# Decoder layer on one core: the gate slots' ring, the tile of the meta rows' sums, and the order around two operand splits

## The chip, the cores and the metric

The kernel runs on one core of a Trainium2 chip. The metric is the device time of one execution in microseconds (us); the time of a kernel is the median of its runs. Engines are named as in the profile: PE is TensorE, DVE is VectorE, ACT is ScalarE, POOL is GpSimd, SP is SyncE, whose queue issues most transfers.

## The reference

One layer of a hybrid decoder on 1024 tokens and 16 meta tokens put in front (T = 1040, D = 1024, feed-forward width 2816), all float32. Cut to what matters:

```python
h = layer_norm(concatenate([meta, x]), in_ln_g, in_ln_b)
z = h @ w_in + b_in          # q | k | v | conv input | 2 x 1024 gate columns
a = swa_sink_attention(q, k, v, sinks, rel_bias)      # window 128, 8 heads, 16 meta keys
y_attn = a @ w_attn_proj                              # 512 -> 1024
c = silu(layer_norm(causal_dwconv(c_val * sigmoid(c_gate), conv_dw, conv_dw_b), ...))
y_conv = c @ w_conv_proj                              # 512 -> 1024
mixed = sigmoid(g_attn) * y_attn + sigmoid(g_conv) * y_conv
h = layer_norm(alpha * h + mixed @ w_out, ln1_g, ln1_b)
u, g = split(causal_dwconv(h @ ffn_w_up, ffn_dw, ffn_dw_b))      # 3 taps
f = (gelu(g) * u) @ ffn_w_down
h = layer_norm(alpha * h + f, ln2_g, ln2_b);  return h[16:]
```

The three-tap convolution of the feed-forward part needs two columns ahead of the first output token, so the kernel carries U = 1026 columns through the second half: the last two meta rows and the 1024 tokens.

## The kernel before, in words

Every matrix product is made in three matmuls: each operand is split into a high part (a cast to the matmul's format, on ACT) and a low part (operand less high part, on DVE, or on POOL where a split isn't urgent), and hi·hi, hi·lo and lo·hi are added up in PSUM (`split`, L268 and L271; `product`, L297, L301 and L302). In the profile a cast with a following `TENSOR_TENSOR` of the same shape is such a split.

The stages, with their place in the profiled span: layer norm and transposes of the input (to about 50 us); the tiles of `w_in`, with attention and the depthwise convolution in between (to about 416); the **projection** (416 to 506); the **output rows** (506 to 605), w_out with residual, layer norm and transposes back; the **joint** to the feed-forward part (605 to 628); the up product (to about 1000) and the down product. All of it is one stream of instructions for each engine, laid down when the program is built by a scheduler that goes by priorities (`rank`) and by the order of dependences; `after(a, b)` and `line` force an order. A wait at the head of an engine's stream holds all that stands behind it.

*Projection.* `for m in range(KC)` makes the 128 output channels of tile m for four groups g of columns (258, 256, 256, 256). A group has two branches of 12 matmuls: attention (operand OA, PSUM tag "mm", three banks) and convolution (operand OC, tag "t", two banks). `merge` then loads both gates of the group from DRAM (tensor `sgd`) into a gate slot on SP's queue, multiplies: L1121 reads and frees the attention bank, L1122 the conv bank, L1123 adds them, and L1128 (ACT) and L1129 (DVE) write the split result into RHC or RHO; L1129 is the slot's last reader. `gslot` hands out the slots: the first four lie in the array FA, then a ring of four in the array OB. The gate loads of a later group therefore wait for the L1129 of the group that had the slot before.

*Meta rows.* The two meta columns of mixed are too few to be worth a matmul. L1125 stores them in `pair`, and `two_rows(k)` adds `pair` times row block k of w_out (128x1024, `wo_raw[k]`) to two sums, one for each meta row: on ACT for k = 0 (L1082), and for k = 1 to 7 by two DVE instructions (L1084). The sums lie in FA (5120 to 6143) and OB (2064 to 3087). Row blocks 0 to 3 of w_out are loaded into FA at the offsets `W_AT`, 4 into FA and 5 into OB, 6 and 7 into buffers `wr`. Places for row blocks 0, 2 and 3 are gate slots before, and the weights of the next m (`wr<-in_w_ab_dram`, split by L268 and by L271 on DVE) go over the same queue.

*Output rows.* `out_rows(i)` makes the tokens of row i in the order 3, 7, 2, -1 (the meta rows), 6, 0, 4, 1, 5, in two halves of 512; L1278 adds the residual and frees the bank, L1300 normalizes, and `turn` (L1314 on PE, L1324 on ACT) transposes the row after the first half of the next one. Between rows, a table `work` lists the splits and sums of operands for the feed-forward part: `split_of` and `form_t2` to `form_t4` make the operands of a product (L1215 the cast, L1220 the low part, L1224 sums), and `w_first(n)` draws n weight operands from the generator `up_weights` (L1362 sums, `wsplit`: L1344 the cast, L1345 the low part).

*Feed-forward.* The up product is made in 2x2 blocks with seven products instead of eight (B11, B21, BT2, BT4, BT1, BT3, B22; PSUM tiles px, pz, px, pw, py, px, py). Tile c = 0 goes in two passes, tokens of the second half first, so that it can begin before all rows are there; its second pass and the splits it needs are the joint. `copy` (L1543, ACT) empties px so that the next product in px can start. The first weight operands lie in W2, which has a pool of its own.

Of the kernel before, what the change touches and what calls it, by code (L numbers as in the profile page):

```python
# [23 lines left out]
F = mybir.dt.float32  # L24
R = mybir.dt.float32r
# [4 lines left out]
P = 128  # L30
D = 1024
# [5 lines left out]
U = T - U0  # L37
# [62 lines left out]
def tile_hybrid_layer(  # L100
# [19 lines left out]
    def after(ins, first):  # L120

        tc.add_manual_dep(ins.ins, first.ins.name, mybir.DependencyInfo(
            mybir.DependencyClass.NoSync, mybir.DependencyReason.SCHED_ONLY), reason="order of work")
# [14 lines left out]
    arena = ctx.enter_context(tc.tile_pool(name="arena", bufs=1, side="left"))  # L138
    dpool = ctx.enter_context(tc.tile_pool(name="scratch", bufs=1, space=bass.MemoryType.DRAM))

    FA = arena.tile([P, 6144], F, name="FA")
    RHC = arena.tile([P, 8320], R, name="RHC")
    RHO = arena.tile([P, 8320], R, name="RHO")
    OB = arena.tile([P, 4 * U + 64], F, name="OB")

    v1d = dpool.tile([NH, J_LEN], F, name="v1d")
    vd = dpool.tile([P, NH, J_LEN], F, name="vd")
# [119 lines left out]
    def split(raw, hi, lo, quick=False, behind=None):  # L267
        ins = nc.scalar.copy(hi, raw)  # L268
        if behind is not None:
            after(ins, behind)  # L270
        return (nc.vector if quick else nc.gpsimd).tensor_tensor(lo, raw, f32(hi), OP.subtract)  # L271
# [437 lines left out]
    for q4 in range(2):  # L709
        ps = pat.tile([P, 512], F, name="ps_v4", tag="t", bufs=2)  # L710
        for i in range(4):
            c = NMETA + (q4 * 4 + i) * P
# [306 lines left out]
    for g in range(3):  # L1019
# [4 lines left out]
    tmp_stack.close()  # L1024
    rx_p = ctx.enter_context(tc.tile_pool(name="rx", bufs=1, side="right", reuse_waits="tile"))
    RX = rx_p.tile([P, 2112], R, name="RX")
    w2_stack, wo_stack = ExitStack(), ExitStack()
    W2 = w2_stack.enter_context(tc.tile_pool(name="w2", bufs=1, side="right", reuse_waits="tile")).tile(
        [P, 2048], R, name="W2")
    wo_p = wo_stack.enter_context(tc.tile_pool(name="rw", bufs=1, side="right", reuse_waits="tile"))  # L1030
    RW = wo_p.tile([P, 2048], R, name="RW")
    RT = OB[:, 0:2048]


# [35 lines left out]
    nc.vector.memset(f32(sel), 0.0)  # L1070
    for t in range(2):
        nc.vector.memset(f32(sel[:, 3 * t:3 * t + 1]), 1.0)
    two_sum = [FA[:, 5120:6144], OB[:, 2064:3088]]
    two_parts = [[OC[:, (2 * t + hl) * D:(2 * t + hl + 1) * D] for hl in range(2)] for t in range(2)]
    wo_raw = {}

# [11 lines left out]
    g_next = [0]  # L1088

    GS = [(FA, i * 516) for i in range(4)]  # L1090
    GS += [(OB, i * 516) for i in range(4)]
    W_AT = (2048, 3072, 0, 1024)

    def gslot():
        i = g_next[0]
        t, o = GS[i if i < 4 else 4 + i % 4]
        g_next[0] += 1
        return t[:, o:o + 516].rearrange("p (i n) -> p i n", i=2)

# [2 lines left out]
    for m in range(KC):  # L1102
        hi, lo = weights([P, KC, P], lambda raw: load(raw, w_ab[m]))

        def branch(i, g, tag, bufs):
            a, b = PG[g]
            ps = pat.tile([P, 512], F, name="ps_p", tag=tag, bufs=bufs)
            rhs = (oo, conv)[i]
            product(ps[:, :b - a], [(hi[:, 4 * i + k], lo[:, 4 * i + k], rhs(k, 0, a, b), rhs(k, 1, a, b))
                                    for k in range(4)])  # L1110
            return ps[:, :b - a]

        def merge(g, psa, psb):
            a, b = PG[g]
            n = b - a
            with rank(RK_EVAC):
                t = gslot()[:, :, :n]
                ins = load(t, dram(sgd, m * P * U + a, [[U, P], [KC * P * U, 2], [1, n]]))

                ta, tb = t[:, 0], t[:, 1]  # L1120
                nc.vector.scalar_tensor_tensor(ta, ta, 1.0, psa, OP.add, OP.mult)  # L1121
                nc.vector.scalar_tensor_tensor(tb, tb, 1.0, psb, OP.add, OP.mult)  # L1122
                nc.vector.tensor_tensor(ta, ta, tb, OP.add)  # L1123
                if g == 0:
                    nc.scalar.mul(pair[:, m, 0:2], ta[:, 0:2], 0.5)  # L1125
                v = ta[:, n - 256:].rearrange("p (t x) -> p t x", t=2)
                h = mixed2(g, m, 0)
                last_act = nc.scalar.mul(h, v, 0.5)  # L1128
                nc.vector.scalar_tensor_tensor(mixed2(g, m, 1), v, 0.5, f32(h), OP.mult, OP.subtract)  # L1129
            return ins, last_act  # L1130

        if m < KC - 1:
            for g in range(4):
                last_gate, last_act = merge(g, branch(0, g, "mm", 3), branch(1, g, "t", 2))
        else:
            pa = [branch(0, g, "mm", 3) if g < 3 else branch(0, g, "s", 2) for g in range(4)]
            for g in range(4):
                last_gate, last_act = merge(g, pa[g], branch(1, g, "t", 2))
        if m in (2, 3):
            raw = (FA[:, 4096:5120], OB[:, 3088:4112])[m - 2]  # L1140
            load(raw, w_out_v[m + 2])
            prep_wo(m + 2, raw, last_act)
        if m < 4:
            early.append(FA[:, W_AT[m]:W_AT[m] + 1024])
            wo_raw[m] = early[m]
            after(load(early[m], w_out_v[m]), last_gate)
        if m > 1:
            with rank(RK_PROJ + 3000):
                two_rows(m - 2)
# [41 lines left out]
    lined, high = [], []  # L1191
# [136 lines left out]
    RING = [RHO[:, i * 1024:(i + 1) * 1024] for i in range(4)]  # L1328
    RING += [None] * 4
    RING += [RHO[:, 6208 + i * 1024:6208 + (i + 1) * 1024] for i in range(2)]  # L1330
    ring_next = [0]

    def wsplit(src):
        i = ring_next[0]
        ring_next[0] += 1
        if i < 2:
            t = W2[:, i * 1024:(i + 1) * 1024]
        else:
            i = (i - 2) % len(RING)
            if RING[i] is None:  # L1340
                RING[i] = wsp_p.tile([P, D], R, name="ws", tag=("whi", "wlo")[i % 2])
            t = RING[i]
        hi, lo = t[:, 0:512], t[:, 512:1024]
        nc.scalar.copy(hi, src)  # L1344
        ins = nc.vector.tensor_tensor(lo, src, f32(hi), OP.subtract)  # L1345
        if pinned_w[0]:
            line(ins)
        elif ring_next[0] <= 12:
            after(ins, formed[0])
        return hi, lo  # L1350
# [7 lines left out]
    def up_weights():  # L1358


        def tt(*x):
            ins = nc.vector.tensor_tensor(*x)  # L1362
            if pinned_w[0]:
                line(ins)

        rows = w_rows(0)
        for c in range(FC):
            a11, a12, a21, a22 = rows
            yield wsplit(a11)
            yield wsplit(a12)  # L1370
            p4 = wsplit(a22)
            tt(a22, a21, a22, OP.add)
            tt(a21, a11, a21, OP.subtract)
            tt(a11, a22, a11, OP.subtract)
            yield wsplit(a11)
            yield p4
            yield wsplit(a22)
            tt(a22, a12, a11, OP.subtract)
            yield wsplit(a21)
            p3 = wsplit(a22)  # L1380
            if c + 1 < FC:
                rows = w_rows(c + 1)
            yield p3
# [17 lines left out]
    def edges():  # L1401
        with rank(RK_TURN):
# [5 lines left out]

    ahead = []
    work = {0: [(w_first, 2), (split_of, 1, B11), (split_of, 1, B21), (split_of, 1, B22)],  # L1410
            4: [(w_first, 3), (split_of, 1, BT2), (form_t4, 1)],
            1: [(form_t3, 1), (split_of, 0, B11, EARLY), (form_t2, 0, EARLY), (w_first, 5)],
            5: [(w_first, 6)]}
    for i in (3, 7, 2, -1, 6, 0, 4, 1, 5):
        if i == -1:
            out_rows(i)
            continue
        rows = out_rows(i, ahead, work.get(i, ()))
        ahead = [None, (i, *rows)] if i == 3 else [(i, *rows)]
        if i == 3:  # L1420
            two_rows(7, rows[2])
        if i == 7:
            for a, (hi, lo) in zip(two_sum, two_parts):
                after(split(a, hi, lo, True), rows[2])
        if i == 0:
            form_t2(1)
        if i == 4:
            split_of(1, BT4)
            split_of(1, BT1)
            edges()  # L1430
        if i == 1:
            split_of(1, BT3)
            split_of(0, B21, EARLY)
            form_t3(0, EARLY)
            form_t4(0, EARLY)
# [1 line left out]


    ps_stack.close()
    wo_stack.close()  # L1440
    up_stack = ExitStack()
    pup = up_stack.enter_context(tc.tile_pool(name="pup", bufs=1, space=PSUM, reuse_waits="tile"))
    ft_next = [0]
# [56 lines left out]
    last_mm, copied = [], []  # L1500
    for c in range(FC):
        if c == 1:
            w2_stack.close()
            sums_p = ctx.enter_context(tc.tile_pool(name="sums", bufs=1, side="right", reuse_waits="tile"))
            RXF, SM1 = (sums_p.tile([P, 2048], F, name=n) for n in ("raw", "sums"))
            for i in range(FC):
                SM[i] = [(OB[:, 2048:4096], SM1)[i % 2][:, h * 1024:(h + 1) * 1024] for h in range(2)]
        V4, X, Z, Y = (pup.tile([P, 1024], F, name=n, tag=n) for n in ("pw", "px", "pz", "py"))
        passes = ((1,), (0,)) if c == 0 else ((0, 1),)
        for subs in passes:  # L1510
# [5 lines left out]
            def at(t, a=a):  # L1516
                return t[:, 254 + a:254 + b]
# [23 lines left out]
            def copy(*x):  # L1541
                with rank(RK_CHAIN):
                    copied.append(nc.scalar.copy(*x))  # L1543

            prod(B11, X, True)
            copy(u13[:, a:b], at(X))
            prod(B21, Z, True)
            if last and c not in (0, FH + 1):
                sums_load(c - 1 if c <= FH else c - 2)
# [277 lines left out]
```

## Time and profile before

| what | value |
|---|---|
| time, median of 3 runs | 1251.87 us (1250.74 to 1251.91) |
| time of the profiled execution | 1253.26 us |
| its span, first to last instruction | 1251.2 us |
| granted TensorE clock, mean | 0.998 |
| PE busy | 1235.7 us, 99% of the span |
| DVE busy | 1092.1 us, 87% |
| ACT busy | 588.7 us, 47% |
| POOL busy | 13.0 us, 1% |
| DMA | 212.10 MB, mean 170 GB/s |

The profile is of one execution. A row of a timeline is: start, duration, engine, line, operation, written tile `<-` read tiles, shape, and in square brackets the idle time of the engine before the row and what released it. DVE and ACT rows overlap a little: the next instruction starts before the last one's record ends, so distances from start to start are shorter than durations. A row of the list of waits is: engine, what it was about to do, what it waited for, us in total, times, longest.

### The profile page before, as it was taken

What the parts mean: (1) busy time and instruction counts of PE and PEld (TensorE: products, weight loads), DVE (VectorE), ACT (ScalarE), POOL (GpSimd) and SP (SyncE); (2) the same over time, 40 slices, a digit from 0 to 9 for tenths busy, and PEclk for the clock granted to TensorE, in tenths of its full rate; (3) what the DMA queues carried; (4) which work ended last, traced back from release to release, by engine and by line L of the source; (5) the groups of instructions that cost most, each with busy time, mean ns of one, the idle gap of its engine ahead of it and who ended that gap; (6) DMA issues with size and microseconds to landing.
All of it is one profiled execution on the core that took longest, in us unless ns stands there. A gap on an engine that the chain in (4) does not pass through costs nothing.

```text
span 1251.2 us, 21661 instructions
## 1 busy us (share of the span) xinstructions
PE 1235.7 (99%) x8514; PEld 1172.0 (94%) x8514; DVE 1092.1 (87%) x1887; ACT 588.7 (47%) x1052; POOL 13.0 (1%) x11
## 2 busy tenths in 40 slices
PE   9999999999999999999999999999999999999997
PEld 8999999999999999888899999999999998888885
DVE  7899989999978778658899999998899986995697
ACT  7522245554566222345565555554555554544330
POOL 0000000000000000100000000000000000000000
PEclk9999999999999999999999999999999999999999
DMA  7294633323244555232146555453464568988722
GB/s 280 67 305 115 184 105 95 104 83 103 68 139 132 175 158 150 84 115 86 68 144 203 181 199 203 177 212 132 156 219 175 197 224 315 393 321 295 252 85 84
DMA packets 98231, 212.10 MB, mean 170 GB/s; under 512 B 12867, under 2 KB 38019, under 8 KB 98002
## 3 DMA queue, kind: packets, MB, share of 16 engines
q1 hardware_dynamic: 86362, 199.65, 47.3%
q10 hardware_dynamic: 11768, 11.08, 2.7%
q8 instruction: 66, 1.08, 0.4%
q14 instruction: 35, 0.29, 0.1%
HBM read 150.30 MB, written 62.70 MB: 170 GB/s over the span
## 4 chain that ended last, share of the span: by engine, by line
PE 90%; DVE 4%; DMA 3%; issue 1%; ACT 1%; SPq 0%; DVEq 0%
PE px L1531 14%; PE py L1531 9%; PE ps_x L1673 9%; PE ps_z L1673 7%; PE ps_z L301 7%; PE ps_z L297 7%; PE ps_z L302 7%; PE pw L1531 5%; PE pz L1531 5%; PE ps_z L513 2%; PE ps_w L302 2%; PE ps_w L297 2%; PE ps_w L301 2%; PE ps_p L297 2%; PE ps_p L302 2%; PE ps_p L301 2%
## 5 line engine op out<-in xcount | busy, mean ns | idle before, releaser
L666 DVE SCALAR_TENSOR_TENSOR FA<-cin,cols,FA 128x1026 f32<-128x1026 f32 x120 | 152.5, 1280 | 0.2
L301 PE MATMUL ps_z<-RHC,whi 128*128 128x384 f32 (+2 forms) x324 | 104.3, 322 | 0.0
L301 PE MATMUL ps_z<-RHO,whi 128*128 128x384 f32 (+2 forms) x324 | 104.3, 322 | 0.0
L297 PE MATMUL ps_z<-RHC,whi 128*128 128x384 f32 (+2 forms) x324 | 104.0, 321 | 0.0
L302 PE MATMUL ps_z<-RHO,wlo 128*128 128x384 f32 (+2 forms) x324 | 103.9, 321 | 0.0
L297 PE MATMUL ps_z<-RHO,whi 128*128 128x384 f32 (+2 forms) x324 | 103.9, 321 | 0.0
L302 PE MATMUL ps_z<-RHC,wlo 128*128 128x384 f32 (+2 forms) x324 | 103.7, 320 | 0.0
L268 ACT CAST whi<-wr 128x1024 fp32r<-128x1024 f32 x37 | 38.9, 1050 | 73.8 <-PE ps_z L301 48.6
L1345 DVE TENSOR_TENSOR RHO<-wr,RHO 128x512 fp32r<-128x512 f32 x92 | 61.9, 683 | 6.1 <-ACT RHO L1344 6.0
L1344 ACT CAST RHO<-wr 128x512 fp32r<-128x512 f32 x92 | 55.2, 619 | 24.7 <-DVE wr L1362 11.2
L297 PEld LDWEIGHTS ps_z<-RHO,whi 128*128 128x128 f32 x324 | 61.0, 188 | 0.5 <-issue 0.3
L302 PEld LDWEIGHTS ps_z<-RHO,wlo 128*128 128x128 f32 x324 | 61.0, 188 | 0.4
L297 PEld LDWEIGHTS ps_z<-RHC,whi 128*128 128x128 f32 x324 | 61.1, 188 | 0.3
L301 PEld LDWEIGHTS ps_z<-RHO,whi 128*128 128x128 f32 x324 | 61.0, 188 | 0.3
L301 PEld LDWEIGHTS ps_z<-RHC,whi 128*128 128x128 f32 x324 | 61.0, 188 | 0.1
L302 PEld LDWEIGHTS ps_z<-RHC,wlo 128*128 128x128 f32 x324 | 60.9, 188 | 0.1
L1362 DVE TENSOR_TENSOR wr<-wr 128x512 f32<-128x512 f32 x88 | 59.9, 681 | 0.2
L673 ACT ACTIVATE FA<-ps_z,cols 128x384 f32<-128x384 f32 (+1 forms) x48 | 26.0, 541 | 47.6 <-PE ps_z L302 43.0
L1543 ACT COPY FA<-px 128x514 f32<-128x514 f32 (+2 forms) x23 | 13.2, 573 | 72.4 <-PE px L1531 72.4
L271 DVE TENSOR_TENSOR wlo<-wr,whi 128x1024 fp32r<-128x1024 f32 x35 | 42.6, 1217 | 4.6 <-ACT whi L268 4.5
L1344 ACT CAST ws<-wr 128x512 fp32r<-128x512 f32 x60 | 36.2, 619 | 18.1 <-DVE wr L1362 10.9
L1531 PE MATMUL px<-OA,RHO 128*128 128x258 f32 (+1 forms) x336 | 43.7, 279 | 0.8 <-ACT OB L1543 0.8
(473 smaller groups left out, 3520.9 us busy)
## 6 DMA issues: line engine op xcount, KB each, us to landing
wr<-in_w_up_dram SPq DMA_DIRECT2D x44, 512.0 KB, 4.5
wr<-in_w_z_dram SPq DMA_DIRECT2D x30, 512.0 KB, 4.0
fd<-FA SPq DMA_DIRECT2D x44, 256.0 KB, 2.5
OB<-in_w_down_dram SPq DMA_DIRECT2D x19, 512.0 KB, 4.8
qt<-qd SPq DMA_DIRECT2D x28, 256.0 KB, 3.6
sgd<-FA ACTq DMA_DIRECT2D x32, 192.0 KB, 4.0
td<-OB SPq DMA_DIRECT2D x12, 512.0 KB
sums<-fd SPq DMA_DIRECT2D x12, 512.0 KB, 7.4
```

The lines of the kernel that those rows point to most:

```text
L268: ins = nc.scalar.copy(hi, raw)
L271: return (nc.vector if quick else nc.gpsimd).tensor_tensor(lo, raw, f32(hi), OP.subtract)
L297: ins = nc.tensor.matmul(ps, ah, bh, start=i == 0, stop=False)
L301: nc.tensor.matmul(ps, ah, bl, start=False, stop=False)
L302: last = nc.tensor.matmul(ps, al, bh, start=False, stop=i == n - 1)
L666: nc.vector.scalar_tensor_tensor(acc[c], cin[:, j:j + U], wc, acc[c], OP.mult, OP.add)
L673: nc.scalar.activation(t, ps, AF.Tanh, bias=bcol(14 + i), scale=0.5)
L1344: nc.scalar.copy(hi, src)
L1345: ins = nc.vector.tensor_tensor(lo, src, f32(hi), OP.subtract)
L1362: ins = nc.vector.tensor_tensor(*x)
L1531: ins = nc.tensor.matmul(o, x[:, ks], bmat(sub, q, hl, k), start=first and k + j == 0, stop=k == 3 and j == 2, skip_group_check=not first)
L1673: nc.tensor.matmul(banks[i], l[:, ts], r[:, ws], start=first and a and x + k == 0, stop=z and x == len(ops) - 1 and k == 2, skip_group_che ...
```

## The change

- The sums of the meta rows get tiles of their own, in a pool `two` that lies next to the pool of RW. FA and OB no longer hold them.
- The ring of gate slots in OB has five slots, not four; OB loses its last 64 columns. The places of w_out's row blocks in FA move by 16, so that none overlaps a first gate slot but those of row blocks 2 and 3.
- W2 has no space from the start. When the sums have been split (after row 7), the pool `two` is closed, and a pool `w2` with W2 takes its space. RW's stack, W2's now too, is closed at c = 1.
- In row 4's list of work, `w_first(3)` is called twice. The generator yields once more (None) for c = 0 after its three sums, so that the first call ends there, the split for BT2 comes next, and the split of the weight sum after it.
- In the joint, the cast for BT1 is ordered behind the copy from px that follows product B11.

```diff
-    OB = arena.tile([P, 4 * U + 64], F, name="OB")
+    OB = arena.tile([P, 4 * U], F, name="OB")
...
-    w2_stack, wo_stack = ExitStack(), ExitStack()
-    W2 = w2_stack.enter_context(tc.tile_pool(name="w2", bufs=1, side="right", reuse_waits="tile")).tile(
-        [P, 2048], R, name="W2")
+    wo_stack, two_stack = ExitStack(), ExitStack()
     wo_p = wo_stack.enter_context(tc.tile_pool(name="rw", bufs=1, side="right", reuse_waits="tile"))
     RW = wo_p.tile([P, 2048], R, name="RW")
+    two_p = two_stack.enter_context(tc.tile_pool(name="two", bufs=1, side="right", reuse_waits="tile"))
...
-    two_sum = [FA[:, 5120:6144], OB[:, 2064:3088]]
+    two_sum = [two_p.tile([P, D], F, name=f"two{t}") for t in range(2)]
...
     GS = [(FA, i * 516) for i in range(4)]
-    GS += [(OB, i * 516) for i in range(4)]
-    W_AT = (2048, 3072, 0, 1024)
+    GS += [(OB, i * 516) for i in range(5)]
+    W_AT = (2064, 3088, 0, 1024)
...
-        t, o = GS[i if i < 4 else 4 + i % 4]
+        t, o = GS[i if i < 4 else 4 + (i - 4) % 5]
...
-            raw = (FA[:, 4096:5120], OB[:, 3088:4112])[m - 2]
+            raw = (FA[:, 4112:5136], OB[:, 3072:4096])[m - 2]
...
-    ring_next = [0]
+    ring_next, W2 = [0], []
...
         if i < 2:
-            t = W2[:, i * 1024:(i + 1) * 1024]
+            t = W2[0][:, i * 1024:(i + 1) * 1024]
...
             tt(a11, a22, a11, OP.subtract)
+            if c == 0:
+                yield None
             yield wsplit(a11)
...
-            4: [(w_first, 3), (split_of, 1, BT2), (form_t4, 1)],
+            4: [(w_first, 3), (split_of, 1, BT2), (w_first, 3), (form_t4, 1)],
...
         if i == 7:
             for a, (hi, lo) in zip(two_sum, two_parts):
                 after(split(a, hi, lo, True), rows[2])
+            two_stack.close()
+            W2.append(wo_stack.enter_context(tc.tile_pool(name="w2", bufs=1, side="right", reuse_waits="tile")).tile(
+                [P, 2048], R, name="W2"))
...
     ps_stack.close()
-    wo_stack.close()
...
         if c == 1:
-            w2_stack.close()
+            wo_stack.close()
...
             copy(u13[:, a:b], at(X))
+            if c == 0 and last:
+                after(high[2], copied[-1])
```

Line numbers of the changed kernel are one lower than before from the meta rows to the output rows (L1084 is L1083, L1121 is L1120), and L1543 is L1546.

How the streams move, at the three places that matter for the prediction. In the orders, ACT's casts read COPY, and DVE's instruction with a scalar and a tensor reads TENSOR_SCALAR.

**Projection, SP's queue.** Before, behind the first gate loads: gates of m = 2 (groups 0 and 1), weights of a later m, gates of groups 2 and 3, then w_out row block 2, and the same again up to the weights ahead of row block 3.

```order
L111 DMA OB<-sgd 128x2x258
L111 DMA OB<-sgd 128x2x256
L111 DMA wr<-in_w_ab_dram 128x1024
L111 DMA OB<-sgd 128x2x256 x2
L111 DMA FA<-in_w_out_dram 128x1024
L111 DMA OB<-sgd 128x2x258
L111 DMA OB<-sgd 128x2x256
L111 DMA wr<-in_w_ab_dram 128x1024
```

After, the gates of group 0 have gone out earlier, and the queue reads:

```order
L111 DMA wr<-in_w_ab_dram 128x1024 x2
L111 DMA OB<-sgd 128x2x256 x3
L111 DMA FA<-in_w_out_dram 128x1024
L111 DMA wr<-in_w_ab_dram 128x1024
L111 DMA OB<-sgd 128x2x258
L111 DMA OB<-sgd 128x2x256 x3
L111 DMA FA<-in_w_out_dram 128x1024
```

The loads of row blocks 2 and 3 now stand behind three gate loads with no weight load between them; a weight load waits for the L271 that frees its buffer.

**Projection, DVE.** Before, from group 1's first multiply in m = 2 (the pair L1084 is row block 2):

```order
L1121 TENSOR_SCALAR OB<-OB,ps_p 128x256
L1129 TENSOR_SCALAR RHO<-OB,RHO 128x2x128
L1122 TENSOR_SCALAR OB<-OB,ps_p 128x256
L1123 TENSOR_TENSOR OB<-OB 128x256
L1121 TENSOR_SCALAR OB<-OB,ps_p 128x256
L1129 TENSOR_SCALAR RHC<-OB,RHC 128x2x128
L1084 TENSOR_SCALAR FA<-FA,pair 128x1024
L1084 TENSOR_SCALAR OB<-FA,pair,OB 128x1024
L1122 TENSOR_SCALAR OB<-OB,ps_p 128x256
L1121 TENSOR_SCALAR OB<-OB,ps_p 128x256
L1122 TENSOR_SCALAR OB<-OB,ps_p 128x256
```

After, from the same multiply:

```order
L1120 TENSOR_SCALAR OB<-OB,ps_p 128x256
L1083 TENSOR_SCALAR two_4560<-FA,pair,two_4560 128x1024
L1083 TENSOR_SCALAR two_4561<-FA,pair,two_4561 128x1024
L1128 TENSOR_SCALAR RHO<-OB,RHO 128x2x128
L1121 TENSOR_SCALAR OB<-OB,ps_p 128x256
L1120 TENSOR_SCALAR OB<-OB,ps_p 128x256
L1122 TENSOR_TENSOR OB<-OB 128x256
L1121 TENSOR_SCALAR OB<-OB,ps_p 128x256
L1122 TENSOR_TENSOR OB<-OB 128x256
```

The pair stood between the multiplies of group 2 and now stands between those of group 1, one group earlier.

**Row 4, DVE.** Before, around the low part for BT2 (OC):

```order
L1345 TENSOR_TENSOR RHO<-wr,RHO 128x512
L1362 TENSOR_TENSOR wr<-wr 128x512 x3
L1345 TENSOR_TENSOR RHO<-wr,RHO 128x512
L1220 TENSOR_TENSOR OC<-OB,OC 128x1024
L1224 TENSOR_TENSOR FA<-OB,FA 128x1024
L1278 TENSOR_TENSOR OB<-ps_w,OB 128x512
```

After:

```order
L1344 TENSOR_TENSOR RHO<-wr,RHO 128x512
L1361 TENSOR_TENSOR wr<-wr 128x512 x3
L1219 TENSOR_TENSOR OC<-OB,OC 128x1024
L1344 TENSOR_TENSOR RHO<-wr,RHO 128x512
L1223 TENSOR_TENSOR FA<-OB,FA 128x1024
L1277 TENSOR_TENSOR OB<-ps_w,OB 128x512
```

The low part of OC and the low part of the weight sum (RHO) have changed places; ACT's order of their casts is as before.

**Joint, ACT.** Before, from the cast for BT2 (OA from OB) on; then those for BT4, BT1 (RX) and BT3:

```order
L1215 COPY OA<-OB 128x1032
L1215 COPY OA<-FA 128x1032
L1215 COPY RX<-FA 128x1024
L1215 COPY OA<-FA 128x1024
L1543 COPY OB<-px 128x258
L1344 COPY RHO<-wr 128x512
```

After:

```order
L1214 COPY OA<-OB 128x1032
L1214 COPY OA<-FA 128x1032
L1546 COPY OB<-px 128x258
L1214 COPY RX<-FA 128x1024
L1214 COPY OA<-FA 128x1024
L1343 COPY RHO<-wr 128x512
```

The copy from px now goes ahead of the casts for BT1 and BT3. Behind this place, in tile c = 1, the first table load and Gelu of the feed-forward part stand ahead of the copy from px of that tile, not behind it, and on PE a few matmuls of the next m's first attention branch go ahead of the last conv branch of m = 1, 2 and 3.

## The prediction

> **What bounds the kernel now.** I read the page's head first, then the list of what TensorE (PE) waits for over the whole run, then the timelines of PE, VectorE (DVE) and ScalarE (ACT) around the waits that lie in changed places.
>
> ```profile
> span 1251.2 us, 21661 instructions
> PE 1235.7 (99%) x8514; PEld 1172.0 (94%) x8514; DVE 1092.1 (87%) x1887; ACT 588.7 (47%) x1052; POOL 13.0 (1%) x11
> PE ps_p L297 <- DVE OB L1122: 2.2, 2, 1.5
> PE ps_h L463 <- DVE xn L427: 1.4, 1, 1.4
> PE ps_w L537 <- DVE sel L1070: 1.1, 1, 1.1
> PE px L1531 <- ACT OB L1543: 0.8, 1, 0.8
> PE ps_s L830 <- DMA qt<-qd: 0.8, 1, 0.8
> PE ps_h L1314 <- DVE OB L1300: 0.6, 1, 0.6
> PE ps_z L510 <- ACT FA L469: 0.3, 1, 0.3
> ```
>
> PE is busy 99% of the span and the change leaves its matmuls as they are. So nothing counts but PE's waits, 7.2 us in seven groups, and waits that the change puts in. Three groups lie where instructions move: the projection's (2.2), the joint's (0.8) and one row's transposes (0.6). No other can go.
>
> **Projection: two late bank releases.** The starts of PE's matmuls tell what the two waits cost.
>
> ```profile
> 465.22 0.28 PE L302 MATMUL ps_p<-OA,wlo 128*128 128x256 f32 x1
> 466.26 0.39 PE L297 MATMUL ps_p<-OC,whi 128*128 128x256 f32 x1 [0.76 <-DVE OB L1122]
> 472.88 0.28 PE L301 MATMUL ps_p<-OA,whi 128*128 128x258 f32 x1
> 474.64 0.39 PE L297 MATMUL ps_p<-OC,whi 128*128 128x256 f32 x1 [1.48 <-DVE OB L1122]
> 449.55 1.28 DVE L1084 SCALAR_TENSOR_TENSOR FA<-FA,pair 128x1024 f32<-128x1024 f32 x1 [2.80 <-DMA FA<-in_w_out_dram]
> 450.75 1.28 DVE L1084 SCALAR_TENSOR_TENSOR OB<-FA,pair,OB 128x1024 f32<-128x1024 f32 x1
> 462.73 1.28 DVE L1084 SCALAR_TENSOR_TENSOR FA<-FA,pair 128x1024 f32<-128x1024 f32 x1 [1.13 <-DMA FA<-in_w_out_dram]
> 469.62 3.10 DVE L1084 SCALAR_TENSOR_TENSOR FA<-FA,pair 128x1024 f32<-128x1024 f32 x1
> 469.14 2.50 POOL L271 TENSOR_TENSOR RW<-OB,RW 128x1024 fp32r<-128x1024 f32 x1 [11.04 <-ACT RW L268]
> 442.65 6.88 DMA FA<-in_w_out_dram
> 457.01 5.69 DMA FA<-in_w_out_dram
> ```
>
> A matmul of 256 columns follows the last by about 0.12 (below), so the waits cost 466.26 - 465.22 - 0.12 = 0.92 and 474.64 - 472.88 - 0.12 = 1.64, 2.56 together. Both end on L1122, which frees a conv bank (two of them), and L1122 stood behind a pair of meta sums (L1084, 1.20 start to start). The pair of w_out block 3 began at 462.73, when its load landed 5.69 after its issue at 457.01. The pair of block 4 needed no load, but its first half lay beside GpSimd's (POOL) 2.50 us split and took 3.10, not 1.28.
>
> **What the change moves there.** With five gate slots, group 0 of the next m finds a free slot, so each gate load needs the group before the one that it needed; the sums' own tiles let w_out block 0 load beside the gates. The w_out loads queue on SyncE (SP) behind gate loads, and come earlier:
>
> ```profile
> 437.45 0.28 PE L297 MATMUL ps_p<-OC,whi 128*128 128x256 f32 x1
> 441.79 0.42 DVE L1129 SCALAR_TENSOR_TENSOR RHC<-OB,RHC 128x256 fp32r<-128x256 f32 x1
> 448.52 0.28 PE L297 MATMUL ps_p<-OC,whi 128*128 128x256 f32 x1
> 459.67 0.28 PE L297 MATMUL ps_p<-OC,whi 128*128 128x256 f32 x1
> ```
>
> Those three PE rows begin the eighth branch of m 1, 2 and 3; 448.52 - 437.45 = 11.07 for 96 matmuls is 0.115 each. Before, block 2's load left at 442.65, just after L1129 of m 1's group 3 ended (441.79 + 0.42). Now the last gate load ahead of it needs L1128 (the same line) of m 1's group 2. By the new order that stands right behind the first multiply of group 3, which is ready when the seventh branch ends (437.45): 437.45 + 0.4 + 0.4 = 438.3, and 0.9 more for two issues (442.65 is 0.44 after 442.21) makes 439.2. Landing 5.69 to 6.88 later: 444.9 to 446.1.
>
> The pair itself stands one group earlier in DVE's order, between the two multiplies of group 1. Behind it wait L1128 (0.42 by L1129's row) and the multiply L1121 (as small), which frees group 1's conv bank, and PE wants that for the conv branch of group 3. That now follows six matmuls of the next attention branch: 448.52 + 6 x 0.12 = 449.2. So block 2's pair must begin by 449.2 - 2.40 - 0.84 = 446.0, and but for 0.1 at the late end it does. It ends by 447.3 to 448.5; seven short instructions later, at most 0.42 each (450.2 to 451.4), a slot is free for m 3, and block 3's load leaves 0.9 after that, 451.1 to 452.3, and lands 456.8 to 459.2. Its limit: seven matmuls ahead, 459.67 + 0.84 - 3.24 = 457.3. PE waits 0 to 1.9; I take 0.5, below the middle, since a load that leaves earlier meets fewer gate loads. Block 4's pair shows no wait for a load. It now starts when m 4's third branch is done and multiplied, 466.26 - 0.92 + 0.4 = 465.8, and even stretched by 3.10 - 1.28 = 1.82 it ends at 470.0; the bank is wanted at 472.88 less the 0.92 that no longer is lost, 472.0, and 0.84 of work lies between. No wait. Blocks 5 to 7 have no PE wait before, and each step comes no later. Sum: -2.56 + 0.5 = **-2.1** (bounds -2.56 and -0.6).
>
> W2, in the sums' old space, is written only when the sums are split: its two casts move on ACT to behind row 3's transposes. By the row of three below they are 0.57 each, 1.1 together, ahead of row 7's transposes, and PE shows no wait for those: nothing; without that cover up to 1.1.
>
> **Row 4's transposes.**
>
> ```profile
> 578.05 1.08 ACT L1215 CAST OC<-OB 128x1024 fp32r<-128x1024 f32 x1
> 578.99 1.70 ACT L1344 CAST RHO<-wr 128x512 fp32r<-128x512 f32 x3
> 580.72 0.69 DVE L1345 TENSOR_TENSOR RHO<-wr,RHO 128x512 fp32r<-128x512 f32 x1 [1.32 <-ACT RHO L1344]
> 581.33 1.22 DVE L1220 TENSOR_TENSOR OC<-OB,OC 128x1024 fp32r<-128x1024 f32 x1
> 586.21 0.81 DVE L1300 TENSOR_SCALAR OB<-OB,mv,sd 128x1024 f32<-128x1024 f32 x1
> 587.16 1.06 PE L1314 MATMUL ps_h<-cols,OB 128*128 128x128 f32 x8 [0.58 <-DVE OB L1300]
> ```
>
> DVE idles 1.32 for the third ACT cast, then makes OC's low part (1.22, of which 0.08 overlaps, as in the pairs above), and L1300 comes late for PE. The added yield splits the work differently, and OC's low part now goes first, into that idle time: its cast is done at 579.13. L1300 then ends 1.1 earlier, at 586.21 + 0.81 - 1.1 = 585.9, before PE is ready for it (587.16 - 0.58 = 586.6). The wait of 0.58 goes: **-0.6**, bounds -0.58 and 0.
>
> **The joint.**
>
> ```profile
> 617.89 1.59 PE L1531 MATMUL pz<-RHO,W 128*128 128x258 f32 x12
> 620.32 1.69 PE L1531 MATMUL px<-OA,RHO 128*128 128x258 f32 x12 [0.83 <-ACT OB L1543]
> 618.01 1.05 ACT L1215 CAST RX<-FA 128x1024 fp32r<-128x1024 f32 x1
> 619.91 0.36 ACT L1543 COPY OB<-px 128x258 f32<-128x258 f32 x1
> 620.28 1.22 DVE L1220 TENSOR_TENSOR OA<-FA,OA 128x1032 fp32r<-128x1032 f32 x1
> 621.42 1.21 DVE L1220 TENSOR_TENSOR RX<-FA,RX 128x1024 fp32r<-128x1024 f32 x1
> ```
>
> PE's product px waits 0.83 for ACT's copy, which stands behind two casts of 0.95. Now the copy goes ahead of them, at 618.0, and px starts when pz is done, 617.89 + 12 x 0.12 = 619.3. But the next product needs the low part that DVE makes from 620.28 to 621.5; it runs 11 matmuls from then, 621.55 + 1.33 = 622.9, and the one after it needs RX's low part, now behind an inserted 258-column sum, 0.42 like L1129: 621.42 + 0.42 + 1.21 = 623.0. Before, it began at 620.32 + 24 x 0.12 = 623.2 and took its second matmul, the first that needs the low part, at 623.35. **-0.4**: DVE is late next. Bounds -0.83 and 0.
>
> Sum: -2.1 - 0.6 - 0.4 = -3.1. The profiled execution took 1253.26 (its span and 2.06 around it) and would take 1250.2; the three runs' median is 1.39 below it, and I take the same waits to be in it, so 1251.87 - 3.1 = **1248.8**.
>
> **A rule against it.** In the up-projection's second tile the order of ACT changes: the copy from px, which came first, now follows a table load and a Gelu.
>
> ```profile
> 630.40 0.59 ACT L1543 COPY OB<-px 128x514 f32<-128x514 f32 x1 [0.17 <-PE px L1531]
> 631.01 1.28 ACT L1461 ACT_TABLE_LOAD   x1
> 632.31 0.63 ACT L1461 ACTIVATE FA<-FA 128x512 f32<-128x512 f32 x1
> 632.94 1.59 PE L1531 MATMUL px<-OA,RHO 128*128 128x258 f32 x12
> ```
>
> Load and Gelu took 632.31 - 631.01 + 0.63 = 1.93; begun at 630.40 - 0.17 - 0.57 = 629.7 (the cast just ahead moves behind them too) they end at 631.6 and the copy at 632.2. PE wants px at 632.94 - 0.4 = 632.5: no wait. The Trainium skill ("ScalarE: Activation LUTs", section "What ACT_TABLE_LOAD costs") gives a switch 1283 ns and a drain of 1380 ns. The trace agrees on the 1.28 and shows no drain behind it, as the Gelu starts 0.02 after the load's end; by the page's drain the copy would end 1.38 later, at 633.6, PE would wait 1.1, and the sum would be -2.0.
>
> **The rivals.**
> - The w_out loads land at the slow end. The load of block 3 then costs PE 1.9, block 2's 0.1, and the joint gives nothing: -2.56 + 2.0 - 0.6 = -1.2, 1250.7. For it: the two landings seen differ by 1.2. Against: both met gate loads issued just ahead. Chance 0.20.
> - Slower: the pairs now stand ahead of a bank release that PE wants sooner. Place: L1083 of blocks 2 and 3. Each us that a landing takes beyond 6.8 (block 2) or 5.6 (block 3, by the middle of its issues, 451.7) is PE's. At 10 us from issue, block 2 costs 439.2 + 10 - 446.0 = 3.2 and block 3 451.7 + 10 - 457.3 = 4.4; with -2.56, -0.6 and -0.4, +4.0: 1255.9. It decides from 8.0 us on, where the sum is nought. For it: three gate loads go just ahead. Against: no landing above 6.88 seen. Chance 0.11.
> - The copy of the second tile holds PE up. If a stretch as long as the load's own 1.28 lies between load and Gelu, the copy ends at 633.5 and PE waits 1.0: -3.1 + 1.0, 1249.8. The Gelu's start at 632.31 speaks against it; that the load stood behind the copy before, where a stall cost PE nothing, leaves it open. Chance 0.04. (The skill's drain, above, is this rival.)
> - The change doesn't reach PE: the loads are held by another item of SP's queue, the waits move but don't shrink, 1251.5. For it: only 3 us of 1251 can go at all. Chance 0.08.
>
> **How the numbers follow.** My forecast has 0.57. A measurement of this kernel tells about 0.2%, 2.5 us, so faster means below 1249.4: 0.54 of the forecast and 0.05 of the first rival make 0.59. Slower, above 1254.4, is the second rival's 0.11. The rest, 0.30, is within. The range's low end is all three waits gone, -2.56 - 0.58 - 0.83 = -4.0, and 0.9 for the spread of runs (1250.74 to 1251.91): 1247.0. Its high end takes the first rival and part of the no-effect case: 1251.2.
>
> **What would show it.** Right: PE's list without L1121 in the projection, or with one wait under 1 on block 3; none on the transposes' L1299; DVE's pairs of blocks 2 and 3 beginning near 445.5 and 457.9; px at the joint near 619.3 with a wait on DVE behind it. Wrong: landings above 7 us, a PE wait on L1121 in m 2 as well as m 3, a px wait at 632.

## The result, and the profile after

The changed kernel took 1249.31 us, median of 15 runs (1248.54 to 1250.80), beside 15 runs of the kernel before with a median of 1252.70. The ratio is 0.9973, 95% interval [0.9966, 0.9981]: 3.4 us faster.

The list of PE's waits of the changed kernel, whole run (columns as before: us in total, times, longest):

```profile
PE ps_h L463 <- DVE xn L427: 1.4, 1, 1.4
PE ps_w L537 <- DVE sel L1069: 1.1, 1, 1.1
PE pw L1534 <- DVE OA L1219: 0.4, 1, 0.4
PE ps_s L830 <- DMA qt<-qd: 0.4, 1, 0.4
PE ps_z L510 <- ACT FA L469: 0.3, 1, 0.3
```

The projection's two waits (2.2), the transposes' (0.6) and the copy's (0.8) are gone; one of 0.4 on the low part in OA is new. The wait on `qt` shrank by 0.4 too, at a place that the change doesn't touch. The weight load that stands just ahead of the first instruction on SP's queue that the change moves comes 0.65 earlier already (first row before, second after):

```profile
398.99 0.34 SPq L111 DMA_DIRECT2D wr<-in_w_ab_dram  x1
398.34 0.35 SPq L111 DMA_DIRECT2D wr<-in_w_ab_dram  x1
```

So I take 0.65 of the 4.1 between the two spans (1251.2 and 1247.1) as difference from one execution to the next, and times of this profile are to be read with 0.65 added when they are set against those of before.

Projection, timelines of SP, DVE and POOL:

```profile
438.20 0.46 SPq L111 DMA_DIRECT2D FA<-in_w_out_dram  x1
450.69 0.46 SPq L111 DMA_DIRECT2D FA<-in_w_out_dram  x1
444.65 2.48 DVE L1083 SCALAR_TENSOR_TENSOR two<-FA,pair,two 128x1024 f32<-128x1024 f32 x2 [1.54 <-DMA FA<-in_w_out_dram]
455.98 2.48 DVE L1083 SCALAR_TENSOR_TENSOR two<-FA,pair,two 128x1024 f32<-128x1024 f32 x2
465.00 2.18 DVE L1122 TENSOR_TENSOR OB<-OB 128x258 f32<-128x258 f32 x1
467.45 2.48 DVE L1083 SCALAR_TENSOR_TENSOR two<-FA,pair,two 128x1024 f32<-128x1024 f32 x2
464.30 2.60 POOL L271 TENSOR_TENSOR RW<-OB,RW 128x1024 fp32r<-128x1024 f32 x1 [8.88 <-DVE wlo L271]
```

The loads of blocks 2 and 3 leave at 438.20 and 450.69, some 4 and 6 us earlier than before. Block 2's pair still waits for its load on DVE, and as in the profile before it doesn't hold PE up; block 3's pair, which held PE up before, finds its data. Block 4's pair takes 2.48: what now lies beside GpSimd's split is the small add L1122, 2.18 long instead of some 0.4.

Row 4, DVE:

```profile
576.16 1.22 DVE L1219 TENSOR_TENSOR OC<-OB,OC 128x1024 fp32r<-128x1024 f32 x1
577.56 0.69 DVE L1344 TENSOR_TENSOR RHO<-wr,RHO 128x512 fp32r<-128x512 f32 x1 [0.19 <-ACT RHO L1343]
581.91 0.81 DVE L1299 TENSOR_SCALAR OB<-OB,mv,sd 128x1024 f32<-128x1024 f32 x1
```

OC's low part fills what was an idle stretch of 1.32; 0.19 of it is left.

Joint, PE, ACT and DVE:

```profile
615.35 1.73 PE L1534 MATMUL px<-OA,RHO 128*128 128x258 f32 x12
616.92 0.28 PE L1534 MATMUL pw<-OA,RHO 128*128 128x258 f32 x1
617.58 1.58 PE L1534 MATMUL pw<-OA,RHO 128*128 128x258 f32 x11 [0.38 <-DVE OA L1219]
614.12 0.38 ACT L1546 COPY OB<-px 128x258 f32<-128x258 f32 x1
616.30 1.22 DVE L1219 TENSOR_TENSOR OA<-FA,OA 128x1032 fp32r<-128x1032 f32 x1
617.78 1.21 DVE L1219 TENSOR_TENSOR RX<-FA,RX 128x1024 fp32r<-128x1024 f32 x1
```

The copy comes in time and px starts without a wait. The next product stops after one matmul until the low part in OA ends at 617.52.

Tile 1, ACT and PE:

```profile
625.83 1.28 ACT L1464 ACT_TABLE_LOAD   x1
627.13 0.63 ACT L1464 ACTIVATE FA<-FA 128x512 f32<-128x512 f32 x1
627.66 0.57 ACT L1546 COPY OB<-px 128x514 f32<-128x514 f32 x1
628.73 1.59 PE L1534 MATMUL px<-OA,RHO 128*128 128x258 f32 x12
```

The copy ends at 628.23, 0.5 before PE's next product in px.

### The profile page after: what moved, and what is told of

It reads as the page before. It is cut to its first block, busy times and chain, and to the rows that moved or that the text cites. A ratio compares the mean times of both kernels' runs of the same rounds, so it can differ in the third digit from the quotient of the medians.

```text
span 1247.1 us, 21668 instructions
## 1 busy us (share of the span) xinstructions
PE 1235.2 (99%) x8514; PEld 1172.2 (94%) x8514; DVE 1093.1 (88%) x1887; ACT 588.8 (47%) x1052; POOL 12.7 (1%) x11
## 4 chain that ended last, share of the span: by engine, by line
PE 94%; DVE 3%; DMA 1%; issue 1%; ACT 0%; SPq 0%; DVEq 0%
PE px L1534 14%; PE py L1534 9%; PE ps_x L1678 9%; PE ps_z L1678 7%; PE ps_z L301 7%; PE ps_z L297 7%; PE ps_z L302 7%; PE pw L1534 5%; PE pz L1534 5%; PE ps_p L302 2%; PE ps_p L297 2%; PE ps_p L301 2%; PE ps_w L302 2%; PE ps_w L297 2%; PE ps_w L301 2%; PE ps_z L513 2%
## 5 line engine op out<-in xcount | busy, mean ns | idle before, releaser
L1361 DVE TENSOR_TENSOR wr<-wr 128x512 f32<-128x512 f32 x88 | 60.0, 682 | 0.2
L271 DVE TENSOR_TENSOR wlo<-wr,whi 128x1024 fp32r<-128x1024 f32 x35 | 42.6, 1216 | 4.6 <-ACT whi L268 4.5
L1546 ACT COPY FA<-px 128x514 f32<-128x514 f32 (+2 forms) x23 | 13.1, 570 | 70.7 <-PE px L1534 70.6
L1344 DVE TENSOR_TENSOR ws<-wr,ws 128x512 fp32r<-128x512 f32 x60 | 40.4, 685 | 4.4 <-ACT ws L1343 4.3
```

## The experiments

**The ring and the pool alone.** The whole change without the two reorderings:

```diff
-            if c == 0:
-                yield None
...
-            4: [(w_first, 3), (split_of, 1, BT2), (w_first, 3), (form_t4, 1)],
+            4: [(w_first, 3), (split_of, 1, BT2), (form_t4, 1)],
...
-            if c == 0 and last:
-                after(high[2], copied[-1])
```

> The ring of five, the sums' own pool and W2 in its space, without the two reorderings in row 4 and at the joint. My theory (three places, each worth its PE wait): both PE waits on L1121 in the projection are gone, the waits of 0.6 on L1299 and of 0.8 on the copy from px stay, and the time falls by 2.6 us (1.0 more than a fifth of the whole remains at the other two places): ratio 0.9979. Rival A (the reorderings are what counts): the projection's waits shrink by less than 1, ratio above 0.9992. Rival B (places work on each other: with the projection earlier, DVE is late elsewhere): a new PE wait of over 0.5 between 500 and 630 us, ratio above 0.9985.

Ratio 0.9980 [0.9971, 0.9989]. From the list of PE's waits:

```profile
PE px L1532 <- ACT OB L1544: 0.9, 1, 0.9
...
PE ps_h L1313 <- DVE OB L1299: 0.6, 1, 0.6
```

No wait in the projection, both others as before, no new one: my theory's figures.

**The reorderings alone**, on the kernel before (the same lines, put in).

> The two reorderings alone, on the kernel before. My theory: the projection keeps its two PE waits (2.2 us in the list of waits), the wait of 0.6 on the transposes goes, the one of 0.8 on the copy from px becomes one of 0.4 on the low part in OA; the time falls by 1.0 us: ratio 0.9992. Rival A: it falls by 2.5 or more. Rival B (nothing at these places reaches the end): no change, ratio 1.0000, and the end of the feed-forward part doesn't move.

Ratio 0.9987 [0.9978, 0.9996]. The interval alone can't part my 0.9992 from rival A (2.5 us, a ratio of 0.998); the waits can. From the list of PE's waits:

```profile
PE ps_p L297 <- DVE OB L1122: 1.5, 1, 1.5
...
PE pw L1533 <- DVE OA L1220: 0.4, 1, 0.4
```

The transposes' wait is gone and the copy's has turned into 0.4 on OA, as expected. In the projection one wait was there in this execution, not two. The 1.5 is block 4's; block 3's hangs on when a load lands. The two parts' effects, 0.20% and 0.13%, add up to the whole 0.27% within their intervals.

**A ring of four in the changed kernel.**

```diff
-    GS += [(OB, i * 516) for i in range(5)]
+    GS += [(OB, i * 516) for i in range(4)]
...
-        t, o = GS[i if i < 4 else 4 + (i - 4) % 5]
+        t, o = GS[i if i < 4 else 4 + (i - 4) % 4]
```

> The whole change, but with a ring of four gate slots. If the ring is what brings the loads of w_out blocks 2 and 3 forward: they go out at about 442 and 456 as before, DVE's pairs for them begin near 449 and 462 with a wait for the load, and PE waits 1 to 2 us in the projection; the time falls by 1.5 to 2.5, ratio 0.9980 to 0.9988. If the sums' own tiles are enough (block 0's load out of the way): the loads go out as early as with five slots, pairs near 445 and 456, no PE wait, ratio 0.9973 as for the whole change.

Ratio 0.9984 [0.9975, 0.9993]. SP's loads of blocks 2 and 3, DVE's pair of block 4, GpSimd's split of RW, and the one projection row of PE's waits:

```profile
441.90 0.46 SPq L111 DMA_DIRECT2D FA<-in_w_out_dram  x1
455.34 0.46 SPq L111 DMA_DIRECT2D FA<-in_w_out_dram  x1
467.44 4.27 DVE L1083 SCALAR_TENSOR_TENSOR two<-FA,pair,two 128x1024 f32<-128x1024 f32 x2
466.96 2.48 POOL L271 TENSOR_TENSOR RW<-OB,RW 128x1024 fp32r<-128x1024 f32 x1 [10.65 <-ACT RW L268]
PE ps_p L297 <- DVE OB L1121: 1.1, 1, 1.1
```

With the sums' own tiles but four slots the loads leave as late as before. So it is the fifth slot that brings them forward. The wait that stays isn't at those blocks, though: it is behind block 4's pair, which takes 4.27 for 2.48. The pair begins 0.5 after GpSimd's split (467.44 and 466.96); with five slots it begins 3.2 after it (467.45 and 464.30) and finds it over. In these two profiles, then, what the fifth slot is worth to PE is the wait at block 4, and the late loads of blocks 2 and 3 cost nothing.

**Who makes block 4's pair long?** First try: in the kernel before, order GpSimd's split of RW behind the pair.

```diff
-        split(raw, hi, lo, k < 4, behind)
+        lo_ins[k] = split(raw, hi, lo, k < 4, behind)
...
+            if k == 4: after(lo_ins[5], ins)
```

> The kernel before, with one edit: GpSimd's low part in RW is ordered behind the pair of w_out block 4, so that the two don't run at the same time. If the shared work with GpSimd made that pair long (3.10 us for its first half): it takes 1.28, the pair ends 1.8 earlier, the PE wait of 1.5 on L1122 near 474 goes, the one of 0.8 near 466 stays, and the time falls by 1.6: ratio 0.9987. If the pair is late for another reason (order alone, or what stands ahead of it): its first half still takes over 2 us or the wait of 1.5 stays, ratio 1.0000.

Ratio 1.0000 [0.9991, 1.0009]. POOL's, DVE's and PE's timelines:

```profile
468.76 2.51 POOL L271 TENSOR_TENSOR RW<-OB,RW 128x1024 fp32r<-128x1024 f32 x1 [10.73 <-ACT RW L268]
469.24 3.11 DVE L1084 SCALAR_TENSOR_TENSOR FA<-FA,pair 128x1024 f32<-128x1024 f32 x1
452.35 0.39 PE L297 MATMUL ps_p<-OC,whi 128*128 128x258 f32 x1 [0.49 <-DVE OB L1122]
465.88 0.39 PE L297 MATMUL ps_p<-OC,whi 128*128 128x256 f32 x1 [0.46 <-DVE OB L1122]
```

This says nothing on the question: `after` (its dependence is marked `NoSync`) only orders what the scheduler lays down, it makes no engine wait for another, and GpSimd ran as early as before: its split begins 0.48 ahead of the pair in both. The two PE rows are the waits behind the pairs of blocks 2 and 3 here.

Second try: RW's low part on DVE, behind m 4's last multiply.

```diff
-        split(raw, hi, lo, k < 4, behind)
+        lo_ins[k] = split(raw, hi, lo, k < 4 or k == 5, behind)
...
-                nc.vector.scalar_tensor_tensor(tb, tb, 1.0, psb, OP.add, OP.mult)
+                conv_mul[m, g] = nc.vector.scalar_tensor_tensor(tb, tb, 1.0, psb, OP.add, OP.mult)
+                (m, g) == (4, 3) and after(lo_ins[5], conv_mul[4, 3])
```

> The kernel before, with the low part in RW made on DVE after m 4's last multiply, not on GpSimd. If GpSimd's instruction made block 4's pair long: its first half takes 1.28 and not 3.10, the PE wait of 1.5 on L1122 near 474 goes, and the time falls by 1.6 less what 1.2 more of DVE work costs (nothing that PE sees): ratio 0.9987. If the pair is late by its place in the order: the wait of 1.5 stays above 1.0, ratio 1.0000. The waits of block 3, which hang on a load, stay at 0 to 0.9.

Ratio 0.9983 [0.9974, 0.9992]. The pair's first half on DVE, and two rows of the list of PE's waits, the projection's and a new one:

```profile
468.51 1.28 DVE L1084 SCALAR_TENSOR_TENSOR FA<-FA,pair 128x1024 f32<-128x1024 f32 x1
PE ps_p L297 <- DVE OB L1122: 0.5, 1, 0.5
PE py L1531 <- ACT OB L1543: 0.2, 1, 0.2
```

The pair stands where it stood in the order and takes 1.28. It begins at 468.51 against 469.62, but of these 1.1 this profile has 0.8 already at the weight load (398.18 for 398.99), and block 3's wait, 0.54 for 0.76, gives 0.2 more. The wait of 1.5 is gone; the 0.5 left is block 3's. One of 0.2 on a copy by ACT, at the joint, is new. So at this place in the order the larger of the projection's two waits comes and goes with GpSimd's split. Moving one instruction off GpSimd is worth about as much as the ring and the pool together (0.9983 and 0.9980).

**Late loads in the changed kernel.** The loads of blocks 2 and 3 go behind the next weight load on SP's queue, and each pair is held ahead of the multiply of group 1, its place in the changed kernel.

```diff
         hi, lo = weights([P, KC, P], lambda raw: load(raw, w_ab[m]))
+        m in (5, 6) and after(early_load[m - 3], last_fill[-1])
...
+            if k in (2, 3): after(conv_mul[k, 1], ins)
```

> The changed kernel, with one thing made late: the loads of w_out blocks 2 and 3 stand behind the next weight load on SyncE's queue (which waits for a split on DVE), and each pair is held ahead of the multiply L1121 of group 1 of its m, where it stands in the changed kernel. My limits (block 2's data by 446.0, block 3's by 457.3, each us beyond is PE's): the loads go out near 441.5 and 454, land 6.4 later, and PE waits for L1121 about 1.8 us in m 2 and 1.4 in m 3, 3.2 together; the ring's gain is gone, ratio 0.9998. Rival (the limits are loose, banks or other work hide a late pair): PE waits under 0.8 together, ratio under 0.9980.

Ratio 0.9977 [0.9968, 0.9986]. SP's load of block 2, the pairs of blocks 2 and 3 on DVE, then the projection's rows in the list of PE's waits:

```profile
442.37 0.46 SPq L111 DMA_DIRECT2D FA<-in_w_out_dram  x1
447.81 2.48 DVE L1083 SCALAR_TENSOR_TENSOR two<-FA,pair,two 128x1024 f32<-128x1024 f32 x2 [1.94 <-DMA FA<-in_w_out_dram]
461.43 2.48 DVE L1083 SCALAR_TENSOR_TENSOR two<-FA,pair,two 128x1024 f32<-128x1024 f32 x2 [1.64 <-DMA FA<-in_w_out_dram]
PE ps_p L297 <- DVE OB L1121: 0.8, 1, 0.8
PE ps_p L297 <- DVE OB L1120: 0.6, 1, 0.6
```

This profile is 0.72 ahead of the one before at the weight load (398.27 for 398.99). With that counted in, block 2's pair began 2.5 beyond my limit of 446.0, and cost PE nothing; block 3's began 4.9 beyond 457.3 and cost 0.8, and 0.6 came later. 1.4 in all, where I had written 3.2 and where my limits, from these starts, would give 7.4. The 0.9998 that I expected lies outside the interval, and the time can't be told from that of the whole change. For block 2 PE's order shows why: the scheduler put 24 attention matmuls ahead of the conv branch in question where it had put 6, some 2 us of work that doesn't need the bank. So the limits hold for one order of PE's work only, and this kernel has another. What a late landing costs in the changed kernel's own order it doesn't show.

**The joint, once more.** In the changed kernel a weight sum (L1361) and a block sum (L1542) stand between low parts for which PE waits. Both are put behind RX's low part (`lows` keeps the low parts by operand; `BT1` is RX's, `B22` the last of the five):

```diff
+            else: loose.append(ins); len(loose) == 1 and after(ins, lows[0, BT1])   # the weight sum
...
+            if c == 0 and last: after(ins, lows[0, BT1])                            # the block sum
```

> The changed kernel, with a weight sum (L1361) and a block sum (L1542) moved behind RX's low part on DVE at the joint. If DVE's order is what holds PE there (0.4 in the list, 0.54 by starts): no wait on pw or py at the joint, the product after px follows without a gap, and the time is 0.5 lower than the changed kernel's: ratio 0.9969 to the kernel before, against 0.9973. Rival: the wait moves to the next operand (RX, or the two that follow) or to tile 1, and the ratio stays 0.9973.

Ratio 0.9967 [0.9955, 0.9980]. PE's fourth product and the low parts that it and the fifth need, on DVE:

```profile
619.84 1.92 PE L1534 MATMUL px<-OA,RHO 128*128 128x256 f32 x12
618.95 2.35 DVE L1219 TENSOR_TENSOR OA<-FA,OA 128x1024 fp32r<-128x1024 f32 x2
```

pw and py follow without a wait now, but the fourth product takes 1.92 where it took 1.52 in the changed kernel, since its low part ends no earlier. px starts at 615.35 in both, and tile 1 at 622.96 and 623.14: 0.18 of 0.54 is won, the rest has moved on, as the rival had it. The ratio can't decide: its interval holds both 0.9969 and 0.9973.

So both sums behind all five low parts (`lows[0, B22]` in place of `lows[0, BT1]`), and the changed kernel again on the same chip:

> As the run before it on the joint, but the weight sum and the block sum go behind the low parts of all five operands on DVE, so that no operand of PE's waits for them. If DVE's order holds PE at the joint: the product pw and the three behind it follow px without a gap, tile 1 begins 0.5 earlier after px than in the changed kernel, ratio 0.9969 to the kernel before where the changed kernel has 0.9973. Rival: the two sums, now late, hold something else up (the first Gelu's input, the copy from px in tile 1, the weights of tile 1), and a new PE wait of over 0.3 stands between 620 and 650.

> The changed kernel again, beside the run above on the same chip: ratio 0.9973 to the kernel before; one PE wait of 0.4 on the low part in OA at the joint, none in the projection; the pair of w_out block 4 takes 2.5 and the add L1122 beside GpSimd's instruction over 2.

1247.62 us (1247.51 to 1248.12, 5 runs), ratio 0.9965 [0.9951, 0.9978], against 1248.89 (1248.04 to 1249.59, 8 runs), ratio 0.9973 [0.9963, 0.9984]. The whole list of PE's waits of the first, and its tile 1:

```profile
PE ps_w L537 <- DVE sel L1069: 1.1, 1, 1.1
PE ps_h L463 <- DVE xn L427: 0.6, 1, 0.6
PE ps_z L510 <- ACT FA L469: 0.3, 1, 0.3
622.00 1.60 PE L1534 MATMUL px<-RHC,ws 128*128 128x258 f32 x12
```

From the first product at the joint to tile 1 it takes 622.00 - 611.98 = 10.02, and 623.23 - 612.39 = 10.84 in the changed kernel. All that PE still waits for lies in the first 20 us. No new wait came with it. This version beats the kernel before; over the changed kernel the profile shows 0.8 at the joint, and seven of its eight runs lie above all five of this version, but the ratios' intervals overlap.

## Why the prediction was right, by its steps

- **PE's waits are the time.** Right: the forecast was -3.1, measured -3.4. (The time itself, 1249.31 for 1248.8, is 0.5 higher, since the kernel before has 1252.70 over 15 runs and not the 1251.87 of the three that I started from.) Between starts of matmuls, 0.92, 1.64 and 0.73 (586.20 to 587.16, less 0.23 for a matmul of 512 columns) went, and 0.99 at the joint (617.89 + 12 x 0.12 to 620.32) became 0.54 (616.92 to 617.58 less 0.12): 3.7 in all, of one execution. Up to tile 1 the two profiles are 3.6 apart (627.36 before and 623.14 after, less the 0.65):

```profile
586.20 0.39 PE L302 MATMUL ps_w<-whi,RHO 128*128 128x512 f32 x1
627.36 1.59 PE L1531 MATMUL px<-RHC,ws 128*128 128x258 f32 x12
623.14 1.60 PE L1534 MATMUL px<-RHC,ws 128*128 128x258 f32 x12
```

- **Where the list doesn't add up.** In the first 13 us. My two profiles of the changed kernel have one span, 1247.1, with 3.6 and 2.4 in their lists of waits. In the second the wait for xn (L463) is 0.59, not 1.44, but the 56 matmuls ahead of it took 8.89, not 7.86. So a difference between two lists in that stretch is none in time.
- **Earlier loads.** Right in place and size: block 2's load left at 438.20, 438.85 with the 0.65, for 439.2; its pair began at 445.3 (444.9 to 446.1). Block 3's left at 451.3 (451.1 to 452.3). The ring of four shows that the fifth slot does it.
- **Block 3's 0.5.** Mis-sized: I took a landing of 5.69 to 6.88. Its pair began 455.98 - 450.69 = 5.3 after the issue without a wait, so the load landed sooner, PE waited nothing, and the first rival didn't come. My reason for taking less than the middle, fewer gate loads, isn't shown: between the two w_out loads SP issued four gate loads in either kernel.
- **Block 3's 0.92 before.** One draw, and the largest seen. In the five kernels with a ring of four the list has 0.76 for it in the kernel before, 0.46 and 0.54 in the two tries on GpSimd's split, and none in the other two; the first of the tries has 0.49 behind block 2's pair besides. A sum from one profile holds such a term only to about 0.5. That the forecast came so near is in part luck: the 0.5 that I kept for block 3 after the change didn't come, the 0.92 before was more than usual, and the two work against each other.
- **Block 4's pair.** The sum was right, the step wasn't. I had it stretched by GpSimd, but early enough at 465.8. It began at 468.1 (with 0.65), since the stretch had fallen on the add ahead of it, and still freed the bank before PE wanted it. That the stretch made the wait, I had not separated from the pair's place; the kernel with the low part on DVE does.
- **The transposes.** Right: L1299 ended at 582.72, 583.4 with the 0.65, or 3.6 before its time in the kernel before, of which 2.5 is the projection's; 1.1 is the step's.
- **The joint.** Right: the copy's wait went and DVE's low part took its place, with the 0.4 named, and the next one (RX) ended just when it was needed.
- **The table load.** The rival didn't come: the copy ended at 628.23, PE wanted 628.73. The load took 1.28 and the Gelu began 0.02 behind it, as before. The drain of 1380 ns that the Trainium skill gives with a switch of tables ("ScalarE: Activation LUTs", section "What ACT_TABLE_LOAD costs") shows in neither trace behind the load.
- **The slower rival.** Its condition didn't come: in all eleven profiles the longest time from the issue of block 2's or 3's load to the pair that waited for it is 449.48 - 442.49 = 6.99 (the first try on GpSimd's split), and it needed 8. Its price stays open. Loads made late by the program cost PE 1.4 and not the 7.4 of my limits, but there PE's order is laid out anew around them.
- **W2.** Nothing, as I had it: the list after has no wait on row 7's transposes.

## What to carry to other kernels

Where the bottleneck engine is busy 99%, list its waits, take the late one's chain back to what releases it, and ask what is late next: the sum of the waits that go, less those that come, was the time here to 0.3 us (3.7 by the starts of matmuls, 3.4 by the medians). A wait behind an instruction that takes longer than its like is first a question of who ran beside it. And an order given to a scheduler makes no engine wait for another: look in the trace whether the edit did what it says.

## What the runs showed of the hardware

While GpSimd makes a 128x1024 low part, a DVE instruction that reads two tensors from SBUF stands still to the end of it: the 258-column add L1122 at 465.00 ended at 467.18, 0.28 after GpSimd (466.90), and block 4's first half in the kernel before at 472.72, 1.08 after GpSimd (471.64). That fits a wait for GpSimd's end, not a slower pace. In all eleven profiles the short DVE instructions (256 or 258 columns) that were held by one of these splits between 450 and 520 ended 0.27 to 0.29 after it, whether they took 0.94 or 2.37. One that began 0.19 after GpSimd's record did (before, 455.42) took its usual 0.42, and one that began 0.31 after it (the changed kernel, 511.99 and 511.68) took 2.36; just when in GpSimd's instruction DVE is held is open. The multiply L1121 just ahead of the add, which reads PSUM and SBUF, ran at its usual length meanwhile (first row; the other two are GpSimd's split and the early DVE instruction of the kernel before):

```profile
464.55 0.41 DVE L1121 SCALAR_TENSOR_TENSOR OB<-OB,ps_p 128x258 f32<-128x258 f32 x1
455.23 2.87 POOL L271 TENSOR_TENSOR RX<-FA,RX 128x1024 fp32r<-128x1024 f32 x1 [451.92 <-DVE OB L1121]
455.42 0.42 DVE L1129 SCALAR_TENSOR_TENSOR RHC<-OB,RHC 128x256 fp32r<-128x256 f32 x1
```
